# A two-block float32 transformer on one core: weight splits around the norms, the order of held products, and which queue carries the other transfers

## The chip, the cores and the metric

The kernel runs on one core of one Trainium2 chip. The metric is the device time of one execution in microseconds (us); lower is better. The core's engines run side by side and meet through semaphores: PE (TensorE) multiplies, DVE (VectorE) and ACT (ScalarE) do elementwise work, POOL is GpSimd, SP (SyncE) only issues transfers. ACT and POOL can issue transfers as well, each in its own queue and in program order.

## The reference

256 tokens of width 1024 pass through two blocks, all in float32:

```python
for layer in range(2):                       # first block
    mix = diff_attention(x) if layer == 0 else stick_breaking(x)
    x = layer_norm(ALPHA * x + mix)
    x = layer_norm(ALPHA * x + peer(x))      # 16384 experts, 16 for each of 8 heads
u = rms_norm(x, attn_pre_norm)               # second block
h = x + rms_norm(hybrid_mixer(u), attn_post_norm)
u = rms_norm(h, mlp_pre_norm)
out = h + rms_norm(square(relu(u @ w_up)) @ w_down, mlp_post_norm)
```

`peer` scores keys, picks experts by two top-16 searches, weighs gelu(x·u) of the picked experts by a softmax and sums their rows of v. The kernel computes it densely: all 16384 rows of u and v, the weights of unpicked experts being zero.

## The kernel before, in words

**Weights as a stream.** All 740 weight tiles (128x1024 float32, 512 KB each) are used once, in the order of `plan`. `Stream.load` brings tile i into one of four `raw` buffers through SP's queue. `Stream.split` makes two float32r parts of it: `hi` by a cast on ACT (line 66), `lo = raw - hi` on DVE (line 67). The activations are split in the same way by `part` (lines 163 and 164), and each product is three matmuls: hi·hi, hi·lo and lo·hi. A raw buffer is free when its `lo` is made, and the next load waits for that. The parts sit in three common buffers (`PARTS`), or, for tiles named by `keep`, in buffers of their own, which need not wait for PE.

**Order.** Each engine works in the order in which the program issues to it. `Stream.next` hands out the tile that is due and, in passing, issues the loads up to three tiles ahead and the splits up to two ahead (plus `extra`), unless all three common buffers are taken.

**Phases.** There are seven: attention 0, peer 0, attention 1, peer 1, mixer, and the two halves of the MLP. Before most of them stands a norm over all 1024 columns, so PE must wait for the vector engines there. The tokens are two blocks of 128 (b = 0, 1). To cover the norm, the last products of a phase for block 1 are held back: for the last `defer` tiles PE does block 0 only, and then the held jobs, 6 matmuls each, for block 1, while DVE and ACT normalise block 0. Then PE transposes block 0 (line 289), does the first four tiles of the next phase for block 0 (`half_pass(0)`, 24 matmuls of 512 columns) while block 1 is normalised, transposes block 1 and does `half_pass(1)`. These four are the junction tiles; they have buffers of their own.

**Where splits are issued.** In `half_pass(0)` each of the four junction tiles is drawn with `next`, which splits two further ahead. In `proj_n` (attention and mixer outputs), `extra` lets all four junction tiles be split before the norm. In the value stage of `peer` (128 tiles of v) `extra` is 0, so two junction tiles are split before the norm, and two junction tiles and the first two tiles after them in `half_pass(0)`, which `layer_norm` issues after the whole norm of block 1.

**Norm.** `norm` adds the residual to the sum in PSUM by halves of 512 columns (line 305), takes mean and variance (308, 309), an inverse root (258 to 264, ACT and DVE in turn), then centres both halves and multiplies by the gain (313), then scales both and adds the bias (316). The second block uses `post_norm` and `pre_norm`, which begin with a sum of squares on ACT (908).

**Other transfers.** The residual `x` is written to DRAM between phases (`spill`) and read again, and gains, masks, tables and sub-keys are loaded, all in SP's queue among the weight tiles. H, the output of the experts' first half, goes out by SP and back in by ACT.

Of the kernel before, what the change touches and what calls it, by code (L numbers as in the profile page):

```python
# [15 lines left out]
ALU = mybir.AluOpType  # L16
# [19 lines left out]
class Stream:  # L36
# [33 lines left out]

    def next(self):

        i = self.used
        self.used += 1
        self.load(i + 1 + self.ahead)
        self.split(i + 1 + self.split_ahead + self.extra, i)
        got = self.cut[i]
        self.cut[i] = None
        return got
# [46 lines left out]
class Kernel:  # L126
# [49 lines left out]

    def mm_n(self, acc, xh, xl, hi, lo, start, stop):

        mm = self.nc.tensor.matmul
        for x, w, a, b in ((xh, hi, start, False), (xh, lo, False, False), (xl, hi, False, stop)):  # L180
            for half in range(2):
                mm(acc[half], x, w[:, half * 512 : half * 512 + 512], start=a, stop=b)  # L182

    def proj_n(self, xh, xl, count, pool, defer, ready=None):


        self.st.keep(count - defer, defer, pool)
        acc, held = None, []
        for k in range(count):
            while ready and not ready(k):  # L190
                self.bg.tick()
            if acc is None:
                acc = [[self.ps("acc") for _ in range(2)] for _ in range(NB)]
            self.st.extra = max(0, min(2, NJ * (k + 2 - count + defer) // defer))
            hi, lo = self.st.next()
            for b in range(NB):
                t = slice(b * P, b * P + P)
                job = (acc[b], xh[:, k, t], xl[:, k, t], hi, lo, k == 0, k == count - 1)
                if b == 0 or k < count - defer:
# [35 lines left out]
    def half_pass(self, b, tiles):  # L235
# [31 lines left out]
    def bcast(self, pool, src, tag):  # L267
        t = pool.tile([P, D], F32, tag=tag, name=f"{tag}{self.n}")
        self.n += 1
        self.nc.sync.dma_start(t, src.unsqueeze(0).to_broadcast([P, D]))  # L270
        return t

    def gains(self, pool, tag, *srcs, late=None):
        t = pool.tile([P, len(srcs), D], F32, tag=tag, name=f"gains{self.n}")
        self.n += 1
        for i, src in enumerate(srcs):
            load = lambda i=i, src=src: self.nc.sync.dma_start(t[:, i], src.unsqueeze(0).to_broadcast([P, D]))
            if late is None:
                load()
            else:  # L280
                late.append(load)
# [13 lines left out]
    def norm(self, pool, b, acc, x, g, beta):  # L295
# [70 lines left out]
    def layer0(self, pool_x):  # L366
        nc, tc, a = self.nc, self.tc, self.a
        with ExitStack() as ctx:
# [166 lines left out]
    def layer1(self, spill):  # L535
        nc, tc, a = self.nc, self.tc, self.a
        mm = nc.tensor.matmul
        with ExitStack() as ctx:
# [5 lines left out]
            mask = one.tile([P, W], F32, tag="mask", name="mask1")  # L544
            nc.sync.dma_start(mask, a["c_mask1"])
            tri = one.tile([P, 2, P], F32R, tag="tri", name="tri1")
            tri_in = one.tile([P, 2, P], F32, tag="tri_in", name="tri_in1")
            nc.sync.dma_start(tri_in, a["c_tri"])
            nc.scalar.copy(tri, tri_in)
# [58 lines left out]
            halves.add(0)  # L608
            nc.sync.dma_start(x, spill)
            for c in range(KD):  # L610
# [15 lines left out]
            j.close()  # L626
            nc.sync.dma_start(spill, x)


    def peer(self, layer, spill, begin):  # L630
# [15 lines left out]
        with ExitStack() as ctx:  # L646
# [5 lines left out]
            sk = rp.tile([P, 8, P], F32, tag="sk", name=f"sk{layer}")  # L652
            nc.sync.dma_start(sk.rearrange("p h n -> p (h n)"), a["sub_keys"][layer])
            nc.sync.dma_start(iota, a["c_iota"])
            nc.sync.dma_start(iotak, a["c_iotak"])
            IX = [rp.tile([P, 2, 16, 8], U16, tag=f"ix{b}", name=f"ix{layer}{b}") for b in range(NB)]
# [184 lines left out]
        with ExitStack() as ctx:  # L841
# [23 lines left out]
            for i in range(P):  # L865
# [8 lines left out]
                if i == P // 2:  # L874
                    xr = vx.tile([P, NB, D], F32, tag="xr", name=f"xr{layer}")
                    nc.sync.dma_start(xr, spill)
# [19 lines left out]
            nc.sync.dma_start(spill, xr)  # L896
            lctx.close()
# [68 lines left out]
    def block2(self, spill):  # L966
# [4 lines left out]
        with ExitStack() as ctx:  # L971
# [7 lines left out]
            sin = one.tile([P, NB, 16], F32, tag="sin", name="sin2")  # L979
            nc.sync.dma_start(cos, a["c_cos2"])  # L980
            nc.sync.dma_start(sin, a["c_sin2"])
            cv = one.tile([P, KD, 8], F32, tag="cv", name="cv2")
            nc.sync.dma_start(cv, a["cols2"])
            mask = one.tile([P, W], F32, tag="mask", name="mask2")
            nc.sync.dma_start(mask, a["c_mask2"])
            qk = [self.jd, kn]
# [193 lines left out]
            x = xp.tile([P, NB, D], F32, tag="x", name="x2")  # L1180
            nc.sync.dma_start(x, spill)
            gains = self.gains(xp, "gains", a["attn_post_norm_2"][0], a["mlp_pre_norm_2"][0])
# [10 lines left out]
        with ExitStack() as ctx:  # L1193
# [6 lines left out]
            for b in range(NB):  # L1200
                self.post_norm(two, acc[b], x[:, b], gains[0])
                u = self.pre_norm(two, x[:, b], gains[1])
                for h in range(2):
                    self.transposed(b, h, u)
                if b == 0:
                    self.half_pass(0, tiles)
            self.half_pass(1, tiles)
            nc.sync.dma_start(spill, x)
        j.close()
        outer.close()  # L1210
        with ExitStack() as ctx:
# [5 lines left out]
            x = one.tile([P, NB, D], F32, tag="x", name="x3")  # L1217
            nc.sync.dma_start(x, spill)
            gain = self.bcast(one, a["mlp_post_norm_2"][0], "gain")
# [25 lines left out]
def body(tc, a, stop="all"):  # L1245
    nc = tc.nc
    with ExitStack() as ctx:
        ctx.enter_context(tc.manual_schedule())
        k = Kernel(tc, ctx, a)
        with tc.tile_pool(name="xa", bufs=1) as px:  # L1250
# [4 lines left out]
            spill = k.dram.tile([P, NB, D], F32, tag="xs", name="xs")  # L1255
            nc.sync.dma_start(spill, x)
        k.peer(0, spill, lambda pool, late: None)
# [99 lines left out]
```

## Time and profile before

| | |
|---|---|
| median of 3 runs | 2309.69 us (2308.02 to 2313.12) |
| the profiled execution's own time | 2311.31 us |
| its span, first to last instruction | 2309.2 us |
| mean granted TensorE clock | 0.988 of full speed |
| busy: PE, DVE, ACT, POOL | 97%, 76%, 54%, 3% |
| moved by DMA | 479.85 MB, mean 208 GB/s |

The span is what the trace covers; 2.1 us of the execution lie outside it. A busy PE in this table is one with a matmul in flight: matmuls overlap, and one that runs at a reduced clock counts as busy for longer.

### The profile page before, as it was taken

What the parts mean: (1) busy time and instruction counts of PE and PEld (TensorE: products, weight loads), DVE (VectorE), ACT (ScalarE), POOL (GpSimd) and SP (SyncE); (2) the same over time, 40 slices, a digit from 0 to 9 for tenths busy, and PEclk for the clock granted to TensorE, in tenths of its full rate; (3) what the DMA queues carried; (4) which work ended last, traced back from release to release, by engine and by line L of the source; (5) the groups of instructions that cost most, each with busy time, mean ns of one, the idle gap of its engine ahead of it and who ended that gap; (6) DMA issues with size and microseconds to landing.
All of it is one profiled execution on the core that took longest, in us unless ns stands there. A gap on an engine that the chain in (4) does not pass through costs nothing.

```text
span 2309.2 us, 39787 instructions
## 1 busy us (share of the span) xinstructions
PE 2230.4 (97%) x15028; PEld 2011.0 (87%) x15028; DVE 1752.8 (76%) x3488; ACT 1237.7 (54%) x2128; POOL 58.3 (3%) x79
## 2 busy tenths in 40 slices
PE   7889999999999999999999999999999899998998
PEld 6769999999888888887999999888888779997987
DVE  5968999888766767576998988766666856676754
ACT  4545454666555444584445566655444546755543
POOL 5400000000000000000000000000000000000000
PEclk9999999999999999999999999999999999999999
DMA  6336667555777777545666655677777564464764
GB/s 209 120 129 226 226 228 241 191 200 203 259 241 259 241 245 252 167 132 179 229 228 229 226 191 201 234 241 243 258 244 249 199 194 149 137 206 142 227 195 142
DMA packets 150657, 479.85 MB, mean 208 GB/s; under 512 B 17728, under 2 KB 18624, under 8 KB 149184
## 3 DMA queue, kind: packets, MB, share of 16 engines
q1 hardware_dynamic: 131456, 442.69, 59.1%
q10 hardware_dynamic: 19008, 34.61, 4.0%
q8 instruction: 118, 1.93, 0.3%
q14 instruction: 75, 0.61, 0.1%
HBM read 437.39 MB, written 39.85 MB: 207 GB/s over the span
## 4 chain that ended last, share of the span: by engine, by line
PE 85%; DVE 6%; ACT 4%; DMA 2%; issue 2%; POOL 1%; SPq 0%; DVEq 0%; ACTq 0%; POOLq 0%
PE ps_acc L182 34%; PE ps_h L157 15%; PE ps_h L159 14%; PE ps_h L158 14%; DVE lo L67 2%; PE ps_acc L805 1%; PE ps_acc L806 1%; ACT hi L66 1%; PE ps_acc L158 1%; PE ps_acc L159 1%; PE ps_acc L157 1%; DMA raw<-w_up 1%; PE ps_acc L689 0%; DVE aa L469 0%; POOL swq L418 0%
## 5 line engine op out<-in xcount | busy, mean ns | idle before, releaser
L67 DVE TENSOR_TENSOR lo<-raw,hi 128x1024 fp32r<-128x1024 f32 x740 | 904.9, 1226 | 454.2 <-ACT hi L66 451.8
L66 ACT CAST hi<-raw 128x1024 fp32r<-128x1024 f32 x740 | 775.4, 1050 | 437.3 <-issue 308.6
L157 PE MATMUL ps_h<-xh,hi 128*128 128x256 f32 x2784 | 790.3, 284 | 5.0 <-ACT r L1237 2.2
L159 PE MATMUL ps_h<-xh,lo 128*128 128x256 f32 x2784 | 774.3, 278 | 1.3 <-DVE lo L67 1.1
L158 PE MATMUL ps_h<-xl,hi 128*128 128x256 f32 x2784 | 774.4, 278 | 0.0
L157 PEld LDWEIGHTS ps_h<-xh,hi 128*128 128x128 f32 x2784 | 526.5, 189 | 11.8 <-ACT r L1237 2.4
L159 PEld LDWEIGHTS ps_h<-xh,lo 128*128 128x128 f32 x2784 | 525.1, 189 | 2.3 <-DVE lo L67 2.3
L158 PEld LDWEIGHTS ps_h<-xl,hi 128*128 128x128 f32 x2784 | 525.3, 189 | 0.2
L182 PE MATMUL ps_acc<-hi,wh 128*128 128x512 f32 x1024 | 315.4, 389 | 3.3 <-ACT wh L163 3.3
L182 PE MATMUL ps_acc<-hi,wo 128*128 128x512 f32 x1024 | 315.4, 389 | 0.0
L182 PE MATMUL ps_acc<-lo,wh 128*128 128x512 f32 x1024 | 315.1, 389 | 0.0
L832 ACT ACTIVATE hs<-ps_h 128x256 f32<-128x256 f32 x256 | 98.3, 384 | 344.1 <-PE ps_h L159 176.2
L182 PEld LDWEIGHTS ps_acc<-hi,wh 128*128 128x128 f32 x1024 | 192.1, 188 | 43.5 <-ACT wh L163 3.6
L182 PEld LDWEIGHTS ps_acc<-hi,wo 128*128 128x128 f32 x1024 | 192.3, 188 | 39.9
L182 PEld LDWEIGHTS ps_acc<-lo,wh 128*128 128x128 f32 x1024 | 192.3, 188 | 39.7
L164 DVE TENSOR_TENSOR wo<-jd,wh 128x256 fp32r<-128x256 f32 x256 | 107.2, 419 | 2.0 <-ACT wh L163 2.0
L856 DVE TENSOR_TENSOR jd<-G,jd 128x256 f32<-128x256 f32 x256 | 106.9, 418 | 2.2 <-ACT G L808 2.2
L163 ACT CAST wh<-jd 128x256 fp32r<-128x256 f32 x256 | 101.7, 397 | 10.4 <-DVE jd L856 10.4
L808 ACT ACTIVATE G<-ps_acc 128x64 f32<-128x64 f32 (+1 forms) x256 | 82.0, 385 | 6.6 <-PE ps_acc L806 1.0
L157 PE MATMUL ps_h<-hi,xh 128*128 128x512 f32 x160 | 70.8, 442 | 11.8 <-ACT hi L66 9.8
L158 PE MATMUL ps_h<-lo,xh 128*128 128x512 f32 x160 | 67.9, 424 | 5.7 <-DVE lo L67 5.7
L159 PE MATMUL ps_h<-hi,xl 128*128 128x512 f32 x160 | 68.0, 425 | 2.5 <-DVE xl L164 2.5
(323 smaller groups left out, 2384.3 us busy)
## 6 DMA issues: line engine op xcount, KB each, us to landing
raw<-peer_u SPq DMA_DIRECT2D x256, 512.0 KB, 4.5
raw<-peer_v SPq DMA_DIRECT2D x256, 512.0 KB, 4.3
H<-hs SPq DMA_DIRECT2D x128, 256.0 KB, 2.1
jd<-H ACTq DMA_DIRECT2D x128, 256.0 KB, 4.2
raw<-w_in SPq DMA_DIRECT2D x32, 512.0 KB, 3.7
raw<-w_up SPq DMA_DIRECT2D x32, 512.0 KB, 4.4
raw<-w_down SPq DMA_DIRECT2D x32, 512.0 KB, 3.7
raw<-w_qkv SPq DMA_DIRECT2D x24, 512.0 KB, 4.5
```

The lines of the kernel that those rows point to most:

```text
L66: self.nc.scalar.copy(hi, raw)
L67: self.nc.vector.tensor_sub(lo, raw, hi)
L157: mm(out, lh, rh, start=start, stop=False)
L158: mm(out, lh, rl, start=False, stop=False)
L159: mm(out, ll, rh, start=False, stop=stop)
L163: self.nc.scalar.copy(hi, src)
L164: self.nc.vector.tensor_sub(lo, src, hi)
L182: mm(acc[half], x, w[:, half * 512 : half * 512 + 512], start=a, stop=b)
L805: mm(out, o[:, 0, j], o[:, 1, j], start=True, stop=False)
L808: nc.scalar.activation(gt[:, :, 4 * g : 4 * g + 4], ps.rearrange("p (t i) -> p i t", t=4)[:, first:end], AF.Copy, scale=1.0 / GSCALE,)
L832: nc.scalar.activation(hs[i // 2][:, i % 2], o, AF.Gelu)
L856: nc.vector.tensor_tensor(w, g[:, i - first], hl[i // 2][:, i % 2], ALU.mult)
```

## The change

Five edits.

1. **Value stage.** From the 116th of the 128 v tiles `extra` is 1, from the 120th 2, so that all four junction tiles are split in the value stage. In `proj_n` the formula for `extra` becomes `k - count + 6`, whatever `defer` is.
2. **Between the norms.** `half_pass(0)` draws its tiles with `calm=True`, which splits no further than the tile itself; before it stands a call that splits all four where that isn't done. `half_pass(1)` splits the next three tiles, one before each of its second, third and fourth steps.
3. **Held products.** `finish` does all held jobs for the first 512 columns, then all for the second.
4. **Norm.** The second half is centred after the first half is finished, not before.
5. **Transfers.** All transfers but weight tiles, H, the first constants and the output go from SP's queue to POOL's (`nc.gpsimd.dma_start`).

```diff
-    def next(self):
+    def next(self, calm=False):
         ...
-        self.split(i + 1 + self.split_ahead + self.extra, i)
+        self.split(i + 1 if calm else i + 1 + self.split_ahead + self.extra, i)
-    def mm_n(self, acc, xh, xl, hi, lo, start, stop):
+    def mm_n(self, acc, xh, xl, hi, lo, start, stop, halves=range(2)):
         ...
-            for half in range(2):
+            for half in halves:
+    def finish(self, held):
+        for half in range(2):
+            for job in held:
+                self.mm_n(*job, (half,))
 # proj_n
-            self.st.extra = max(0, min(2, NJ * (k + 2 - count + defer) // defer))
+            self.st.extra = max(0, min(2, k - count + 6))
         ...
-        for job in held:
-            self.mm_n(*job)
+        self.finish(held)
 # half_pass
             if b == 0:
-                tiles.append(self.st.next())
+                tiles.append(self.st.next(calm=True))
+            elif j:
+                self.st.split(self.st.used + j, self.st.used)
 # norm
-        for s in halves:
-            nc.vector.scalar_tensor_tensor(y[:, s], y[:, s], mv[:, 0:1], g[:, s], ALU.subtract, ALU.mult)
+        centre = lambda s: nc.vector.scalar_tensor_tensor(y[:, s], y[:, s], mv[:, 0:1], g[:, s], ALU.subtract, ALU.mult)
+        centre(halves[0])
         next(root)
         for s in halves:
+            if s is halves[1]:
+                centre(s)
             nc.vector.scalar_tensor_tensor(x[:, b, s], y[:, s], r, beta[:, s], ALU.mult, ALU.add)
 # layer_norm, ahead of half_pass(0); the same in block2
+        self.st.split(self.st.used + NJ, self.st.used)
 # peer, value stage
+                if i >= GSPLIT:
+                    self.st.extra = min(2, (i - GSPLIT) // 4)
                 hi, lo = self.st.next()
         ...
-            for job in held:
-                self.mm_n(*job)
+            self.st.extra = 0
+            self.finish(held)
 # layer0, and so for gains, bcast, mask, tri_in, sk, iota, iotak, xr, cos, sin, cv, x and spill elsewhere
-            nc.sync.dma_start(x, a["x"].rearrange("(b p) d -> p b d", p=P))
+            nc.gpsimd.dma_start(x, a["x"].rearrange("(b p) d -> p b d", p=P))
```

## Rows read from the trace of the kernel before

**Rows 1.** The page, busy time, share and count by engine.
```profile
PE 2230.4 (97%) x15028; PEld 2011.0 (87%) x15028; DVE 1752.8 (76%) x3488; ACT 1237.7 (54%) x2128; POOL 58.3 (3%) x79
```

**Rows 2.** Windows over three junctions: length, busy by engine, PE clock, DMA.
```profile
905.00:945.00 40.00, 35.39 (x155) 27.77 (x154) 28.90 (x49) 14.85 (x25) 0.00 (x0) 0.96 0.53 177
1795.00:1860.00 65.00, 58.07 (x239) 45.45 (x238) 47.52 (x94) 30.38 (x52) 0.14 (x2) 0.92 0.54 180
2098.00:2150.00 52.00, 41.53 (x223) 34.57 (x222) 30.21 (x58) 24.84 (x50) 0.00 (x0) 0.90 0.46 162
```

**Rows 3.** Timeline of PE, peer 0 to attention 1: start, length, [idle before].
```profile
929.33 0.50 PE L157 MATMUL ps_h<-hi,xh 128*128 128x512 f32 x1 [1.53 <-ACT hi L66]
932.44 0.73 PE L158 MATMUL ps_h<-lo,xh 128*128 128x512 f32 x1 [2.60 <-DVE lo L67]
```

**Rows 4.** Timeline of DVE in the same junction.
```profile
915.41 1.27 DVE L305 SCALAR_TENSOR_TENSOR lny<-xr,ps_acc 128x512 f32<-128x512 f32 x2
...
923.18 0.69 DVE L305 SCALAR_TENSOR_TENSOR lny<-xr,ps_acc 128x512 f32<-128x512 f32 x1 [1.58 <-PE ps_acc L182]
924.46 0.69 DVE L164 TENSOR_TENSOR xl<-ps_m,xh 128x512 fp32r<-128x512 f32 x1 [0.59 <-ACT xh L163]
```

**Rows 5.** Timeline of ACT: the last value tiles, and the start of attention 1.
```profile
908.72 1.05 ACT L66 CAST hi<-raw 128x1024 fp32r<-128x1024 f32 x1 [0.95 <-DMA raw<-peer_v]
...
945.98 0.41 ACT L549 CAST tri<-tri_in 128x256 fp32r<-128x256 f32 x1
```

**Rows 6.** Timeline of SP there: spill, mask and table in its queue.
```profile
932.79 0.43 SPq L896 DMA_DIRECT2D xs<-xr  x1
...
939.64 0.43 SPq L548 DMA_DIRECT2D tri_in<-c_tri  x1
```

**Rows 7.** Timeline of PE, peer 1 to mixer.
```profile
1828.98 1.09 PE L289 MATMUL ps_m<-ident,pnu 128*128 128x128 f32 x8 [1.68 <-DVE pnu L925]
...
1844.25 1.06 PE L289 MATMUL ps_m<-ident,pnu 128*128 128x128 f32 x8 [0.93 <-DVE pnu L925]
...
1858.36 0.51 PE L158 MATMUL ps_acc<-lo,xh 128*128 128x512 f32 x1 [0.95 <-DVE lo L67]
```

**Rows 8.** Timeline of DVE in the same junction.
```profile
1819.87 1.27 DVE L305 SCALAR_TENSOR_TENSOR lny<-xr,ps_acc 128x512 f32<-128x512 f32 x2
...
1824.64 1.42 DVE L316 SCALAR_TENSOR_TENSOR xr<-lny,lnr,gains 128x512 f32<-128x512 f32 x2
...
1828.43 0.48 DVE L925 TENSOR_SCALAR pnu<-pnu,pnr 128x512 f32<-128x512 f32 x1
...
1837.00 4.62 DVE L67 TENSOR_TENSOR lo<-raw,hi 128x1024 fp32r<-128x1024 f32 x4
```

**Rows 9.** Timeline of PE, attention 0 to peer 0, and attention 1 to peer 1.
```profile
150.67 1.82 PE L289 MATMUL ps_m<-ident,x 128*128 128x128 f32 x8 [2.29 <-DVE x L316]
...
162.01 0.50 PE L159 MATMUL ps_h<-hi,xl 128*128 128x512 f32 x1 [1.09 <-DVE xl L164]
...
1065.93 0.50 PE L159 MATMUL ps_h<-hi,xl 128*128 128x512 f32 x1 [1.41 <-DVE xl L164]
```

**Rows 10.** Timeline of the mixer-to-MLP junction: DVE, PE, SP.
```profile
2115.77 2.36 DVE L67 TENSOR_TENSOR lo<-raw,hi 128x1024 fp32r<-128x1024 f32 x2 [0.26 <-ACT hi L66]
...
2125.05 1.94 PE L289 MATMUL ps_m<-ident,pnu 128*128 128x128 f32 x8 [3.77 <-DVE pnu L925]
...
2134.53 0.33 SPq L1218 DMA_DIRECT2D x<-xs  x1
...
2145.64 0.39 PE L157 MATMUL ps_h<-xh,hi 128*128 128x256 f32 x1 [2.20 <-ACT r L1237]
```

**Rows 11.** Timeline of DVE at the end of the program.
```profile
2301.95 1.41 DVE L938 TENSOR_TENSOR qnu<-ps_acc,gain 128x512 f32<-128x512 f32 x2 [4.03 <-ACT msj L908]
```

**Rows 12.** Rows of the page's transfers, and POOL's tile in attention 0.
```profile
x<-x SPq DMA_DIRECT2D x1, 1024.0 KB, 6.1
L418 POOL TENSOR_TENSOR swq<-zq,sin x32: 712/733/1692, 26.1 to 90.8; 32x256 f32<-32x256 f32 x32
```

More of the change, by code (lines that the diff above doesn't have):

```diff
@@ L269, in bcast @@
         self.n += 1
-        self.nc.sync.dma_start(t, src.unsqueeze(0).to_broadcast([P, D]))
+        self.nc.gpsimd.dma_start(t, src.unsqueeze(0).to_broadcast([P, D]))
         return t
@@ L276, in gains @@
         for i, src in enumerate(srcs):
-            load = lambda i=i, src=src: self.nc.sync.dma_start(t[:, i], src.unsqueeze(0).to_broadcast([P, D]))
+            load = lambda i=i, src=src: self.nc.gpsimd.dma_start(t[:, i], src.unsqueeze(0).to_broadcast([P, D]))
             if late is None:
@@ L544, in layer1 @@
             mask = one.tile([P, W], F32, tag="mask", name="mask1")
-            nc.sync.dma_start(mask, a["c_mask1"])
+            nc.gpsimd.dma_start(mask, a["c_mask1"])
             tri = one.tile([P, 2, P], F32R, tag="tri", name="tri1")
             tri_in = one.tile([P, 2, P], F32, tag="tri_in", name="tri_in1")
-            nc.sync.dma_start(tri_in, a["c_tri"])
+            nc.gpsimd.dma_start(tri_in, a["c_tri"])
             nc.scalar.copy(tri, tri_in)
@@ L608, in layer1 @@
             halves.add(0)
-            nc.sync.dma_start(x, spill)
+            nc.gpsimd.dma_start(x, spill)
             for c in range(KD):
@@ L626, in layer1 @@
             j.close()
-            nc.sync.dma_start(spill, x)
+            nc.gpsimd.dma_start(spill, x)
     def peer(self, layer, spill, begin):
@@ L652, in peer @@
             sk = rp.tile([P, 8, P], F32, tag="sk", name=f"sk{layer}")
-            nc.sync.dma_start(sk.rearrange("p h n -> p (h n)"), a["sub_keys"][layer])
-            nc.sync.dma_start(iota, a["c_iota"])
-            nc.sync.dma_start(iotak, a["c_iotak"])
+            nc.gpsimd.dma_start(sk.rearrange("p h n -> p (h n)"), a["sub_keys"][layer])
+            nc.gpsimd.dma_start(iota, a["c_iota"])
+            nc.gpsimd.dma_start(iotak, a["c_iotak"])
             IX = [rp.tile([P, 2, 16, 8], U16, tag=f"ix{b}", name=f"ix{layer}{b}") for b in range(NB)]
@@ L875, in peer @@
                     xr = vx.tile([P, NB, D], F32, tag="xr", name=f"xr{layer}")
-                    nc.sync.dma_start(xr, spill)
+                    nc.gpsimd.dma_start(xr, spill)
                 if i >= GSPLIT and (i - GSPLIT) % 4 == 2 and late:
@@ L895, in peer @@
             self.layer_norm(tp, acc, xr, gb, bb, extra(tp, xr) if extra else None)
-            nc.sync.dma_start(spill, xr)
+            nc.gpsimd.dma_start(spill, xr)
             lctx.close()
@@ L979, in block2 @@
             sin = one.tile([P, NB, 16], F32, tag="sin", name="sin2")
-            nc.sync.dma_start(cos, a["c_cos2"])
-            nc.sync.dma_start(sin, a["c_sin2"])
+            nc.gpsimd.dma_start(cos, a["c_cos2"])
+            nc.gpsimd.dma_start(sin, a["c_sin2"])
             cv = one.tile([P, KD, 8], F32, tag="cv", name="cv2")
-            nc.sync.dma_start(cv, a["cols2"])
+            nc.gpsimd.dma_start(cv, a["cols2"])
             mask = one.tile([P, W], F32, tag="mask", name="mask2")
-            nc.sync.dma_start(mask, a["c_mask2"])
+            nc.gpsimd.dma_start(mask, a["c_mask2"])
             qk = [self.jd, kn]
@@ L1180, in block2 @@
             x = xp.tile([P, NB, D], F32, tag="x", name="x2")
-            nc.sync.dma_start(x, spill)
+            nc.gpsimd.dma_start(x, spill)
             gains = self.gains(xp, "gains", a["attn_post_norm_2"][0], a["mlp_pre_norm_2"][0])
@@ L1205, in block2 @@
                 if b == 0:
+                    self.st.split(self.st.used + NJ, self.st.used)
                     self.half_pass(0, tiles)
             self.half_pass(1, tiles)
-            nc.sync.dma_start(spill, x)
+            nc.gpsimd.dma_start(spill, x)
         j.close()
@@ L1217, in block2 @@
             x = one.tile([P, NB, D], F32, tag="x", name="x3")
-            nc.sync.dma_start(x, spill)
+            nc.gpsimd.dma_start(x, spill)
             gain = self.bcast(one, a["mlp_post_norm_2"][0], "gain")
@@ L1255, in body @@
             spill = k.dram.tile([P, NB, D], F32, tag="xs", name="xs")
-            nc.sync.dma_start(spill, x)
+            nc.gpsimd.dma_start(spill, x)
         k.peer(0, spill, lambda pool, late: None)
```

## The prediction, made before the result was known

> **What bounds the kernel now.** I read the page's busy times first: PE has a matmul in flight for 97% of the span [rows 1], with a fixed list of matmuls that the change does not touch. So time is to be had only where PE waits or runs at its lower clock. The timeline of PE, read for its idle times, shows them at the junctions. The windows put sizes on three of them [rows 2]: PE is idle for 4.6 of 40 us, 6.9 of 65 and 10.5 of 52, and the mean granted clock is 0.96, 0.92 and 0.90. The clock has two levels, 2.4 and 1.2 GHz, so a mean of 0.90 over 52 us is 10.4 us at the lower one, in which PE does half the work: 5.2 us lost beside the idle time, and 5.2 and 1.6 us in the other two windows. Then I took the timelines of DVE and ACT at each junction to see what stood ahead of the late instruction. It is mostly splits: PE waits for hi and lo of junction tiles that were issued behind block 1's norm [rows 3], for a pre-norm behind four lo [rows 7, 8], for xl behind two lo of the next phase [rows 9], or for a post-norm behind two [rows 10]. So the working goes junction by junction.
>
> **The change part by part.** *Peer 0 to attention 1.* The splits leave half_pass(0), and with them the idle 1.53 and 2.60 [rows 3] and the fall of the clock behind them (1.6): -5.7. But the two splits now stand ahead of block 0's norm on DVE. Four lo take 4.62 [rows 8], so two take 2.3, which is the lower bound of how late that norm starts. The loads may add to it: in this stretch ACT already waited 0.95 once for a tile [rows 5], and tiles are now asked for faster. Two such waits make the upper bound, 4.2. I take 3.1, between them, since only the last tiles can outrun the loads. What hides it: behind block 0's norm DVE sat idle for 1.58, until the held products were done, and for 0.59 [rows 4]. That covers 2.2, and 0.9 stays (0.1 to 2.0): -4.8 in all.
>
> The earlier end of the held half (edit 3) gives nothing here or at any other junction: DVE comes to that sum after the products are done. Edit 4 brings the first half of x one operation earlier, 0.7 (two take 1.42 [rows 8]), but the third matmul behind the transposes needs xl, which DVE makes after both halves of x; here that takes the gain.
>
> *The table of attention 1.* ACT casts tri at 945.98 [rows 5]; the copy of the first k is queued behind it, and with it a PSUM bank that PE needs for its third projection. The table was asked for 6.9 us after the spill was issued (932.79 to 939.64 [rows 6]), because its memory was the spill's source. Block 1's norm, and so the spill, comes no earlier, while ACT reaches the cast some 5 us earlier. PE's first two projections cover part. How long GpSimd takes to issue a transfer is in no row; nothing, if it issues as SP does and the cover is enough, and 4 us, the whole lead less about 1, are the ends. I take +1.6, nearer to the lower end, as two projections are about that much work.
>
> *Peer 1 to mixer.* The same two splits: late by 2.6 (2.3 to 3.5; the norm was started by a late load here already). Nothing hides it, since PE waits 1.68 for the pre-norm as it is [rows 7]. Then the four lo between block 1's norm and its pre-norm go: 4.6 [rows 8], less 0.4 of the pre-norm's squares on ACT that ran beneath them; the pre-norm's own 2.85 (1826.06 to 1828.91 [rows 8]) remains. The second transposes come at +2.6 - 4.6 + 0.4 = -1.6. half_pass(0) begins 2.6 later but no longer stalls for its tiles, so PE is through with it sooner and waits some 2 us for them in place of 0.93 [rows 7]. That may bring the lower clock, as it followed the idle times of attention 1's junction at a price of 1.6: 0 to 1.6, I take 0.9. And the wait of 0.95 for lo at the start of the mixer [rows 7] goes, as those tiles are split in half_pass(1): -0.9. Together -1.6 (-2.5 to +1).
>
> *Attention 0 to peer 0, attention 1 to peer 1.* The idle 1.09 and 1.41 before L159 [rows 9] were lo of the next phase ahead of xl; they go to half_pass(1), whose products outlast them. Edit 4 takes 0.7 from the idle 2.29 before the transposes, and one split that moves to an earlier step 0.2; in the second, of which less reaches PE, 0.5. -2.0 and -1.9 (each +-1, with the clock).
>
> *Mixer to MLP.* The norm of block 0 starts where it did: the order among its splits is the same. For block 1 two lo, 2.36, stood ahead of the post-norm [rows 10]: -2.4 of the idle 3.77, and 1.4 is left. With that the second stretch at the lower clock, about half of this window's 5.2 lost, shortens or goes: -1.6 (0 to -2.6). The wait of 2.20 at 2145.64 [rows 10] is a weight tile whose load was queued on SP behind x, and x was issued only at 2134.53, when half_pass(1) had freed its memory; on POOL's queue only the gain stands behind x: -2.2. Together -6.2.
>
> By the Trainium skill's page "DMA: Bandwidth & Descriptors", section "Issuing engines are not separate DMA queues", all queues run on the same 16 engines and another issuer saves only the issue time. By that alone these 2.2 would stay and the sum would be 2.2 smaller. What the row shows is a wait ahead of an issue, which bandwidth does not set, so I count them.
>
> *End and start.* At the end the first half of block 1 is done 18 matmuls earlier, so one of two squares and one of two products (1.41 for both [rows 11]) leave the tail: -0.7. At the start the load of x, on SP behind the first weight tiles, has no transfer ahead of it on POOL and meets the first weights and x transposed. It takes 6.1 for itself [rows 12]; half of that, 3.0, is the upper bound and nothing the lower. PE begins at the lower clock, where a delay costs half: +0.8.
>
> *Other transfers.* Residual, gains, masks and sub-keys within the long stages are covered by the weight tiles that are loaded three ahead; on POOL they go out as soon as their memory is free. If that cover fails, where the residual meets the first tiles of the two value stages, it costs up to 1 each; I take nothing. In the value stage the two further splits fall into DVE's spare time (76% busy [rows 1]); their price at its end is counted above.
>
> **Sum.** -4.8 + 1.6 - 1.6 - 2.0 - 1.9 - 6.2 - 0.7 + 0.8 = -14.8. From the profiled execution's own 2311.3 that is 2296.5. That execution lies 1.6 above the median of the runs shown, so a median would be near 2295; I say 2296.
>
> **Rivals.** *GpSimd's transfers come late* (the other side). Between 26 and 91 us one instruction of POOL takes between 712 and 1692 ns [rows 12] at the same size, so POOL can be held up while DVE works. If what it issues lands D later than from SP, four places pay, as their consumers stand in order on an engine that PE waits for: the table of attention 1 (ACT), cos and sin of the mixer (DVE), and the sub-keys of both peers (PE itself). With about 2 us of cover each, the cost is 4 x (D - 2): the whole gain is gone at D = 5.7, and at 8 the time is 2311.3 - 14.8 + 24 = 2320. For it: nothing in this trace says what D is. Against: DVE idles often at the junctions. I give it 6%. The Trainium skill's page "SBUF — State Buffer", sections "SBUF: two separate sides" and "Who interferes with whom", states why it could be: GpSimd writes descriptors through a port pair that it shares with DVE, and cannot while DVE runs in a two-port mode; it advises the queues of ACT or SP. No run here shows that yet.
>
> *The value stage only exchanges one wait for another.* If the loads cannot follow, the norm is late by 4.2 at both value ends. Then peer 0 gives -3.7 + 1.6, peer 1 +1, and PE's longer wait for the transposes costs the lower clock twice, 1.6 each. With the other terms (-10.0) the sum is -7.9: about 2303. For it: ACT's wait for a load in just this stretch [rows 5]. Against: one wait of 0.95 only. 22%.
>
> *Nothing comes of it*: PE's waits go where they were, but DVE, now the last at each junction, opens others of the same size and the lower clock follows them; 2307 to 2311. Against: DVE is idle for 24% of the span, and at the MLP junction its work gets shorter, not later. 9%, of which 1 for slower.
>
> The forecast keeps 63%: 2290 to 2302 by its own terms. The range of 2288 to 2304 takes in most of the second rival and leaves out the first, the third and the tails. A change under 0.2%, 4.6 us, is about what a measurement of this kernel can't tell from none. Faster than that: 0.85, the same 0.08, slower 0.07.
>
> **What would show it.** Right: no wait for hi or lo in half_pass(0) of attention 1's start; block 0's norm starting 2.3 to 4.2 later against the end of its products at both value ends; the idle time before L159 gone at both entries to peer; the idle before the second transposes of the MLP junction at about 1.4; no wait for r at the MLP's third tile; a wait of ACT for tri_in. Wrong: DVE or ACT waiting several us for anything issued by POOL, idle time of PE within a value stage, or half-clock stretches as long as before.

## The result, and the profile after

The changed kernel takes 2296.96 us (median of six executions, 2292.23 to 2298.80) against 2309.0 for the kernel before, run beside it: a ratio of 0.9939, 95% interval 0.9924 to 0.9955. The forecast was 2296 (2288 to 2304), faster by more than 0.2%. The profiled execution of the changed kernel took 2292.23, of which the trace spans 2290.5; it is the quickest of its six, 4.7 under their median, so part of what its trace shows is chance. A second profile, below, helps to tell which part.

The page's busy time after, against [rows 1]:

```profile
PE 2219.0 (97%) x15028; PEld 2000.7 (87%) x15028; DVE 1755.9 (77%) x3488; ACT 1239.7 (54%) x2128; POOL 77.3 (3%) x114
```

The matmuls are as many as before, and POOL has 35 more instructions, its transfers. PE is busy for 11.4 us less: it spends less time at the lower clock, and its matmuls of 256 columns were quicker by chance, as shown below. The windows that hold the work of [rows 2], with the same columns:

```profile
903.56:939.20 35.64, 34.85 (x160) 26.78 (x159) 30.42 (x52) 16.88 (x26) 2.93 (x6) 1.00 0.56 198
1785.69:1849.08 63.39, 57.74 (x238) 45.50 (x237) 49.88 (x99) 32.02 (x53) 2.81 (x7) 0.92 0.55 189
2086.18:2131.42 45.24, 38.82 (x223) 32.70 (x222) 32.28 (x59) 26.02 (x52) 1.59 (x3) 0.96 0.56 194
```

PE's idle time falls from 4.6 to 0.8 us in the first, little (6.9 to 5.7) in the second and from 10.5 to 6.4 in the third; the clock goes from 0.96, 0.92 and 0.90 to 1.00, 0.92 and 0.96.

Both kernels issue 15028 matmuls, and the order differs only among held products. So the start of the n-th matmul before, less its start after, is the lead that the changed kernel has there, and its growth over a stretch is what the stretch gave. The table has the stretches by the times of the kernel before, with the forecast's terms; plus is a gain, and the second profile is the one of the next section:

```
stretch (us, before)                     forecast   first profile   second profile
start, to 30                                -0.8         -2.8            -0.7
attention 0 to peer 0, 100 to 172           +2.0         +3.5            +2.2
peer 0 to attention 1, 900 to 940           +4.8         +5.0            +4.8
table of attention 1, 940 to 960            -1.6         -1.8            -1.5
attention 1 to peer 1, 1045 to 1070         +1.9         +1.4            +0.3
peer 1 to mixer, 1780 to 1865               +1.6         +1.6            -1.0
mixer to MLP, splits and norm, 2090 to 2141 +4.0         +3.8            +1.6
the same, wait for r, 2141 to 2150          +2.2         +2.9            +2.7
end, after 2295                             +0.7         +0.2            +0.2
all long stages between (six stretches)      0           +5.0            +0.2
sum                                        +14.8        +18.8            +9.0
```

The timeline of PE in the changed kernel, peer 0 to attention 1 [rows 3] and the start of attention 1, with all idle times over 0.2:

```profile
924.28 0.51 PE L157 MATMUL ps_h<-hi,xh 128*128 128x512 f32 x1 [0.24 <-ACT xh L163]
931.33 0.63 PE L296 MATMUL ps_m<-ident,xr 128*128 128x128 f32 x4 [0.48 <-DVE xr L325]
944.58 0.39 PE L157 MATMUL ps_h<-xh,hi 128*128 128x256 f32 x1 [1.28 <-ACT k L622]
```

The waits for hi and lo inside the first half pass, 1.53 and 2.60, are gone; the last line is new, the price of the table of attention 1. The same view, peer 1 to mixer [rows 7] (two lines) and mixer to MLP [rows 10] (two lines):

```profile
1822.06 1.97 PE L296 MATMUL ps_m<-ident,pnu 128*128 128x128 f32 x8 [3.16 <-DVE pnu L937]
1833.73 1.07 PE L296 MATMUL ps_m<-ident,pnu 128*128 128x128 f32 x8 [2.19 <-DVE pnu L937]
...
2100.95 1.97 PE L296 MATMUL ps_m<-ident,pnu 128*128 128x128 f32 x8 [3.96 <-DVE pnu L937]
2111.30 1.07 PE L296 MATMUL ps_m<-ident,pnu 128*128 128x128 f32 x8 [1.96 <-DVE pnu L937]
```

At peer 1 the idle times only moved: 1.68 to 3.16 ahead of block 0's transposes, 0.93 to 2.19 ahead of block 1's, and the wait of 2.61 for a lo inside the half pass, at 1838.27 in the kernel before, is gone. At the MLP 3.77 fell to 1.96 and the 2.20 for r is gone.

### The profile page after: what moved, and what is told of

The parts are those of the page before. It is cut to its first block, busy times and chain, and to the rows that moved or that the text cites. A ratio compares the mean times of both kernels' runs of the same rounds, so it can differ in the third digit from the quotient of the medians.

```text
span 2290.5 us, 39880 instructions
## 1 busy us (share of the span) xinstructions
PE 2219.0 (97%) x15028; PEld 2000.7 (87%) x15028; DVE 1755.9 (77%) x3488; ACT 1239.7 (54%) x2128; POOL 77.3 (3%) x114
## 4 chain that ended last, share of the span: by engine, by line
PE 82%; DVE 7%; issue 4%; ACT 4%; DMA 2%; POOL 1%; SPq 0%; ACTq 0%; DVEq 0%; POOLq 0%
PE ps_acc L182 31%; PE ps_h L157 14%; PE ps_h L159 14%; PE ps_h L158 14%; DVE lo L67 2%; ACT hi L66 1%; PE ps_acc L815 1%; PE ps_acc L816 1%; PE ps_acc L158 1%; PE ps_acc L157 1%; PE ps_acc L159 1%; DMA raw<-w_v 1%; PE ps_acc L699 0%; DVE aa L479 0%; POOL swq L428 0%
## 5 line engine op out<-in xcount | busy, mean ns | idle before, releaser
L163 ACT CAST wh<-jd 128x256 fp32r<-128x256 f32 x256 | 101.7, 397 | 10.6 <-DVE jd L866 10.5
L157 PE MATMUL ps_h<-hi,xh 128*128 128x512 f32 x160 | 69.0, 431 | 10.5 <-ACT hi L66 8.9
L815 PE MATMUL ps_acc<-oh 128*128 128x128 f16 x512 | 69.6, 221 | 0.0
L816 PE MATMUL ps_acc<-oh 128*128 128x128 f16 x512 | 68.6, 219 | 0.0
```

The source lines that it names most:

```text
L157: mm(out, lh, rh, start=start, stop=False)
L163: self.nc.scalar.copy(hi, src)
L815: mm(out, o[:, 0, j], o[:, 1, j], start=True, stop=False)
L816: mm(out, o[:, 0, j], o[:, 2, j], start=False, stop=True)
```

## Experiments

The theory: the gain is made at the junctions, by edit 2 above all (when splits are issued between the norms), and the queue pays at the MLP and costs at the start. The rivals: the queue carries it, or edit 1 does, or the splits only exchange one wait for another.

### Both kernels once more

No edit.

> The changed kernel once more, for a second profile and more times. Its first profile was the fastest of its six executions (2292.2 against a median of 2297.0) and leads the kernel before by 18.8 us, of which 13 to 14 lie at the junctions. The rest lies elsewhere: twice 1.3 in the key stages (experts' first half), 1.6 and 0.9 from two falls of the clock in the attention of layer 1 and the mixer that it does not have, and -0.9 in attention 0. Theory: these five are chance, so this profile has other values there and the same ones at the junctions (start +2.8, peer 0 to attention 1 -4.9 with +1.8 for the table, peer 1 to mixer -1.6, mixer to MLP -6.7, each within 0.5); median 2297 within 2. Rival: the 1.3 twice belong to the change, as other transfers left SP's queue, and come again.

> The kernel before once more, for a second profile. Theory: its junctions repeat to 0.3 us; what differs are falls of the clock and the rate of the 256-column matmuls at full clock, which was 113 ns each in some long stages and 118 in others, the same stage differing from execution to execution (up to 2.6 us in the first half of the MLP, 1.3 in a key stage). Rival: the rate belongs to the kernel (where its code or its tiles lie), so this profile has the same rate in each stage as the first of this kernel: 118 in the second part of both key stages, 113 in the MLP.

Measured: the changed kernel 2298.48 (2293.89 to 2301.99), ratio 0.9938 (0.9922 to 0.9954), profiled in 2301.99. The kernel before took 2316.53 in one execution. The second column of profiles above is this changed kernel against the first trace of before. Peer 0 (4.8), the table (1.5) and r (2.7) repeat within 0.4. The start, peer 1 to mixer and the splits at the MLP do not (-0.7, -1.0 and 1.6 in place of -2.8, 1.6 and 3.8), so the expectation that all junctions repeat within 0.5 failed at three of them. At peer 1 both profiles have the same time at the lower clock, and the norm of block 0 comes later in the second, as shown under the value stage. At the MLP the second has one more fall of the clock. Such falls follow the same idle time in one execution and not in the next; the windows of both profiles at attention 1 to peer 1, the first execution first:

```profile
1045.00:1060.00 15.00, 12.46 (x59) 9.31 (x59) 13.59 (x29) 4.71 (x10) 0.54 (x1) 1.00 0.20 75
```

```profile
1045.00:1060.00 15.00, 12.75 (x55) 9.71 (x54) 13.01 (x28) 4.96 (x10) 0.54 (x1) 0.89 0.23 94
```

Idle before the transposes was 1.19 and 0.87 in the first, 1.15 and 0.87 in the second; still one ran on at 1.00 and the other at 0.89 over 15 us. That is 15 x 0.11 = 1.7 us of work lost, more than the difference between +1.4 and +0.3. About half of the 9.8 between the two profiles is the rate of matmuls of 256 columns. Windows in the first half of the MLP, changed kernel (first and second execution), then before (first and second):

```profile
2131.50:2171.50 40.00, 40.00 (x356) 40.00 (x355) 29.66 (x46) 23.70 (x45) 0.00 (x0) 1.00 0.65 197
```

```profile
2139.00:2179.00 40.00, 40.00 (x342) 40.00 (x341) 28.10 (x44) 23.19 (x44) 0.00 (x0) 1.00 0.64 188
```

```profile
2150.00:2190.00 40.00, 40.00 (x355) 40.00 (x355) 30.64 (x47) 24.78 (x47) 0.00 (x0) 1.00 0.71 207
```

```profile
2153.00:2193.00 40.00, 40.00 (x342) 40.00 (x341) 28.02 (x43) 23.11 (x44) 0.00 (x0) 1.00 0.63 188
```

355 or 342 matmuls in 40 us, at the full clock and with PE never idle: one every 113 ns or every 117. Each kernel has had both rates in this stage, so the rate belongs to the execution; it is worth 2.5 us here and 1.3 in a key stage, where the first profile of the changed kernel was quick twice. So the rivals of both expectations fall: the 1.3 did not come again, and the kernel before did not keep its rates. But of the five differences that were taken for chance one came again: between 960 and 1045 the first profile gains 1.6 and the second 1.5. It goes with the table, as shown there.

### The load of x back on SP

```diff
 # layer0
-            nc.gpsimd.dma_start(x, a["x"].rearrange("(b p) d -> p b d", p=P))
+            nc.sync.dma_start(x, a["x"].rearrange("(b p) d -> p b d", p=P))
```

> Changed kernel, only the load of x in attention 0 back on SP's queue. Theory: on GpSimd's queue it goes out at 1.35 us and shares the engines with the first weight tiles, which costs PE 1.8 of idle time and a fall of the clock by 18.8 us; on SP it stands behind the first weight tiles, so PE's waits of 1.03 and 0.75 go and the time falls by 2.8, to about 2294. Rival: the first tiles are late for another reason, or x collides on SP as well; 2297 and the same two waits.

Measured: 2294.93 (2291.16 to 2298.68), ratio 0.9929 (0.9912 to 0.9945). By the medians it is 2.0 to 3.6 quicker than the changed kernel; by the intervals it can't be told from it. The traces tell more. PE's waits at the start in the changed kernel, first profile (two lines) and second (one):

```profile
17.05 0.51 PE L157 MATMUL ps_h<-hi,xh 128*128 128x512 f32 x1 [1.03 <-ACT hi L66]
18.31 0.50 PE L158 MATMUL ps_h<-lo,xh 128*128 128x512 f32 x1 [0.75 <-DVE lo L67]
```

```profile
17.77 0.50 PE L158 MATMUL ps_h<-lo,xh 128*128 128x512 f32 x1 [0.29 <-DVE lo L67]
```

With x on SP there is none after the first 10 us of this stage. In the changed kernel x goes out at 1.35 us, among the first weight tiles, and takes 11.5 to land where it took 6.1 [rows 12]. Leads at 20 us over the first trace of before: with x on SP +0.5 to +0.7 in four other kernels and -0.4 in the second profile of before; with x on POOL -0.4 to -0.7 in five profiles and -2.8 in the first. The means, without that one, are +0.3 (six profiles, the first of before at 0 among them) and -0.6: the usual price is about 0.9 us, and the 2.8 that the theory took from one profile was mostly chance.

### All transfers back on SP

`nc.gpsimd.dma_start` becomes `nc.sync.dma_start` in all 20 places; edits 1 to 4 stay.

> Changed kernel with all transfers of edit 5 back on SP's queue; edits 1 to 4 stay. Theory: the queue gives 2.2 to 2.9 at the MLP's third tile (a wait for r that comes back) and takes 2.8 at the start; the table of attention 1 is worth no more than 1 either way: 2297 within 2. Rival A, the queue carries more of the gain (the key stages' 1.3 twice, weight tiles no longer held up behind other transfers): 2300 or more. Rival B, GpSimd's issue costs time at each junction: 2294 or less.

Measured: 2301.01 (2296.91 to 2303.36), ratio 0.9949 (0.9933 to 0.9964). By the medians rival A has the size, 2.5 to 4 us for the queue, though the intervals overlap; it does not have the place that it named, the key stages. The trace shows four places: r at the MLP, the start of the mixer, the start of the program and the table of attention 1. PE's wait for r at the MLP is back, and two waits at the start of the mixer:

```profile
1851.61 0.51 PE L157 MATMUL ps_acc<-hi,xh 128*128 128x512 f32 x1 [0.79 <-ACT hi L66]
1852.87 0.50 PE L158 MATMUL ps_acc<-lo,xh 128*128 128x512 f32 x1 [0.75 <-DVE lo L67]
...
2134.18 0.39 PE L157 MATMUL ps_h<-xh,hi 128*128 128x256 f32 x1 [2.37 <-ACT r L1250]
```

SP's own timeline says why: at both places four weight tiles stand behind transfers that waited for memory or for the spill.

```profile
1842.63 0.33 SPq L992 DMA_DIRECT2D cos<-c_cos  x1
...
1845.70 1.86 SPq L50 DMA_DIRECT2D raw<-w_qkv  x4
...
2122.92 0.33 SPq L1231 DMA_DIRECT2D x<-xs  x1
2123.29 0.43 SPq L277 DMA_DIRECT2D gain<-mlp_post_norm  x1
2123.76 2.25 SPq L50 DMA_DIRECT2D raw<-w_up  x4
```

Against the second profile of the changed kernel the two profiles differ by 4.5 in the stretch of r (a fall of the clock of 1.7 in it) and 1.7 at peer 1 to mixer for the queue, and by 1.3 at the start and 1.5 at the table against it: 3.5 in all at these four places (the two spans differ by 1.3 alone, as other stretches went the other way). The table is a place where POOL's queue loses. In the changed kernel POOL issues it after the mask, and ACT waits; the timelines of POOL and of ACT, and the table's KB and time to landing:

```profile
936.81 0.54 POOL L555 DMA_DIRECT2D mask<-c_mask  x1 [4.79 <-DMA xs<-xr]
937.34 0.54 POOL L558 DMA_DIRECT2D tri_in<-c_tri  x1
```

```profile
943.85 0.41 ACT L559 CAST tri<-tri_in 128x256 fp32r<-128x256 f32 x1 [4.28 <-DMA tri_in<-c_tri]
```

```profile
tri_in<-c_tri POOLq DMA_DIRECT2D x1, 128.0 KB, 6.3
```

With all queues back on SP (its timeline, then ACT's, then the transfers' KB and time to landing):

```profile
933.51 0.43 SPq L558 DMA_DIRECT2D tri_in<-c_tri  x1
```

```profile
937.36 0.41 ACT L559 CAST tri<-tri_in 128x256 fp32r<-128x256 f32 x1
```

```profile
tri_in<-c_tri SPq DMA_DIRECT2D x1, 128.0 KB, 2.3
```

2.3 us to landing in place of 6.3, and no wait. The weight tiles that SP's queue held back there had been issued ahead of the table in the changed kernel.

### The table alone on POOL, and the table on SP

In the first, the load of x and of both gains of attention 1 go back to SP, mask and table stay on POOL. In the second, the load of x in attention 0 and that of the table go to SP:

```diff
 # table alone: layer1
-            nc.gpsimd.dma_start(x, spill)
+            nc.sync.dma_start(x, spill)
         ...
 # table (and x of layer0, as above) on SP: layer1
-            nc.gpsimd.dma_start(tri_in, a["c_tri"])
+            nc.sync.dma_start(tri_in, a["c_tri"])
```

> Changed kernel with the load of x and of the two gains of attention 1 on SP's queue, so that mask and table are the only transfers that GpSimd issues there. In the changed kernel the table landed 6.1 to 6.3 us after its issue, as the second of five in a row; from SP's queue 2.3. Theory: the five share what carries them, so alone the table lands in 3 to 4 and PE's wait for k is below 0.3. Rival: GpSimd is late with it whatever follows (its issue, or DVE's work beside it): 5.5 or more and PE's wait of about 1 stays.

> Changed kernel with two transfers back on SP's queue: the load of x in attention 0 and the table of attention 1; the other transfers stay on GpSimd's. Theory: from GpSimd's queue the table landed 6.1 to 6.3 us after its issue, from SP's 2.3 (all queues back) to 3.4, and with all queues back ACT's cast of it kept PE waiting for nothing; so the wait for k (1.07 to 1.28) goes and with it 1.5 us at the start of attention 1, beside the 1 to 3 of x at the start: about 2293.5. Rival: the table waits for the spill to land, whatever the queue, and PE's wait stays at 1 us: 2295, as with x alone.

Measured, table alone: one execution of 2298.36; PE's wait for k is 1.84. Its transfers and ACT's cast stand as in the rival: 6.6 us to landing. But neither reading fits: x, issued from SP at 935.32, lands ahead of it after 4.8. The transfers:

```profile
x<-xs SPq DMA_DIRECT2D x1, 1024.0 KB, 4.8
raw<-w_q SPq DMA_DIRECT2D x2, 512.0 KB, 7.4
...
mask<-c_mask POOLq DMA_DIRECT2D x1, 192.0 KB, 6.3
tri_in<-c_tri POOLq DMA_DIRECT2D x1, 128.0 KB, 6.6
```

Here, in the changed kernel and with the queues back, transfers land nearly in the order in which they were issued, whichever queue they came from; POOL reaches the mask 0.9 after the spill has landed, and by then x and a weight tile are ahead. That a transfer is not slow because GpSimd issues it shows at the start of the mixer, where at most one weight tile is under way: a mask of 192 KB lands about as soon from either queue (changed kernel, then queues back).

```profile
mask<-c_mask POOLq DMA_DIRECT2D x1, 192.0 KB, 2.6
```

```profile
mask<-c_mask SPq DMA_DIRECT2D x1, 192.0 KB, 2.3
```

Measured, table on SP: 2294.98 (2290.27 to 2297.53), ratio 0.9930 (0.9917 to 0.9944). The table lands in 2.1, ACT does not wait, and the stretch from 940 to 960 loses nothing (the changed kernel: 1.5 to 1.8). In the median the 1.5 over x alone is not to be seen; intervals of 3 us to either side could not show it.

And part of the 1.5 is given back later. In all twelve profiles PE idles for the same 2.1 us near 1025 (times of before). Where PE has waited for k (five profiles), and in one more, the one without edits 3 and 4, its clock then stays at 1.00 and the stretch from 960 to 1045 gains 1.5 to 1.6. In the other six the clock falls there, and the stretch gains nothing. The windows over that place, x alone on SP and then x and table on SP, which differ in the table's queue alone:

```profile
1010.00:1030.00 20.00, 17.90 (x93) 15.42 (x93) 15.60 (x27) 15.29 (x28) 0.00 (x0) 1.00 0.34 101
```

```profile
1010.00:1030.00 20.00, 17.90 (x87) 15.45 (x86) 14.03 (x24) 13.97 (x27) 0.00 (x0) 0.91 0.32 89
```

In four of the six profiles without that fall one comes at the next junction, attention 1 to peer 1, where the stretch then gives -0.3 to 0.3 in place of 1.1 and 1.4. So from 940 to 1070 the six give 0.1 to 1.2 in sum, and the three kernels with edit 2 and the table on SP 1.5 to 2.2. Why a loss of 0.4 to 2.2 us at the table does away with a fall of the clock 80 us later, no run shows.

The kernel with x and table on SP and the one with x alone there have lower medians than the changed kernel and are the quickest versions found, though their intervals overlap its own.

### The splits undone, and edit 2 alone

In the first, edits 1 and 2 are undone. In the second, edit 2 alone is put into the kernel before:

```diff
 # edit 2 alone; next takes calm as in the change
         ...
-                tiles.append(self.st.next())
+                tiles.append(self.st.next(calm=True))
+            elif j:
+                self.st.split(self.st.used + j, self.st.used)
 # layer_norm and block2, ahead of half_pass(0)
+        self.st.split(self.st.used + NJ, self.st.used)
```

> Changed kernel with edits 1 and 2 undone: splits are issued where they were before; held products by halves, norm and queues stay as changed. Theory: the splits are most of the gain: +4.9 at peer 0 to attention 1 less 1.7 of the table's wait, +1 to 2 at each entry to a peer, +1.6 at peer 1 to mixer, +3 to 4 at mixer to MLP: +10 to +12, so 2307 to 2309. Rival (the value stage only exchanges one wait for another, and the splits between norms only move DVE's work): 2301 or less.

> Kernel before with edit 2 alone: calm draws in half_pass(0), the call that splits all four junction tiles ahead of it, three further tiles in half_pass(1). Value stage, held products, norm and queues as before. Theory: this is the part that carries the gain: 1 at each entry to a peer (no lo of the next phase ahead of xl), 4 at peer 0 to attention 1 without the table's wait, 0 to 1 at peer 1 to mixer, 3 to 4 at mixer to MLP, where the wait for r stays: 9 to 11 of the 12 to 14, so 2299 to 2302. Rival: it needs edit 1 (junction tiles split ahead of the norm) or the queue to pay; 2304 or more.

Measured: 2307.51 without the splits (2304.66 to 2312.01, ratio 0.9984, 0.9974 to 0.9993), 2298.75 with edit 2 alone (2298.37 to 2302.59, ratio 0.9952, 0.9940 to 0.9965). The theory held in both (edit 2 alone is even 0.25 us under its bracket): edits 1 and 2 are three quarters of the gain, 0.46% of 0.62, and edit 2 without any other makes 0.48%. Without the splits the waits of [rows 3] are back:

```profile
928.51 0.50 PE L157 MATMUL ps_h<-hi,xh 128*128 128x512 f32 x1 [1.53 <-ACT hi L66]
931.75 0.51 PE L158 MATMUL ps_h<-lo,xh 128*128 128x512 f32 x1 [2.74 <-DVE lo L67]
```

With edit 2 alone, other transfers on SP, the start of the mixer still has a wait for lo of 0.76, and the MLP one for r of 1.65.

### The value stage without edit 1

```diff
                 if i >= GSPLIT:
-                    self.st.extra = min(2, (i - GSPLIT) // 4)
+                    self.st.extra = 0
```

> Changed kernel with edit 1 undone in the value stages alone: no splits further ahead there, so two junction tiles are split between the norms of the two blocks (two lo, 2.4 us) and not before the first norm. Edit 2 stays. Theory: in the last six steps of the value stage PE needs 1.36 us a step and DVE 1.81 with a lo in each, so the further two lo make PE fall behind (0.8 to 1.4 at peer 0, 1.9 at peer 1) and delay the norm by about 3; without them the first norm starts earlier, and the two lo delay the second block's pre-norm by 2.4 in its place: net -1 to +1 at each end, so 2295 to 2299; edit 2 carries nearly all of the gain at the value ends. Rival: edit 1 carries it, and hi or lo of junction tiles make PE wait in the first half pass again: 4 to 8 slower, 2301 to 2305.

Measured: 2296.52 (2292.58 to 2299.01), ratio 0.9937 (0.9925 to 0.9950): the same as the changed kernel, as the theory had it. Against PE's work (its start, plus the lead that PE had before the last steps of the stage, less the start in before) the norm of block 0 starts 0.7 later than in the kernel before at both peers, where the changed kernel starts it 3.0 and 3.1 later at peer 0 and 2.3 and 4.4 at peer 1 (its two profiles). PE's waits, peer 0 (two lines) and peer 1 (two lines):

```profile
928.13 0.63 PE L296 MATMUL ps_m<-ident,xr 128*128 128x128 f32 x4 [1.74 <-DVE xr L325]
929.58 0.63 PE L296 MATMUL ps_m<-ident,xr 128*128 128x128 f32 x4 [0.82 <-DVE xr L325]
...
1820.47 1.09 PE L296 MATMUL ps_m<-ident,pnu 128*128 128x128 f32 x8 [2.17 <-DVE pnu L937]
1833.96 1.94 PE L296 MATMUL ps_m<-ident,pnu 128*128 128x128 f32 x8 [6.03 <-DVE pnu L937]
```

Two lo stand ahead of the norm or behind it, and PE waits ahead of block 0's transposes or of block 1's. The stretch at peer 0 gives 4.0 where the changed kernel gives 4.8 to 5.0, that at peer 1 +0.4 where five profiles with edit 1 and these transfers on POOL give 1.6, -1.0, 1.0, 2.3 and 0.3. What edit 1 costs shows in the value stage, in ACT's timeline of the changed kernel, where ACT waits for loads:

```profile
901.55 1.05 ACT L66 CAST hi<-raw 128x1024 fp32r<-128x1024 f32 x1 [0.81 <-DMA raw<-peer_v]
...
904.32 1.05 ACT L66 CAST hi<-raw 128x1024 fp32r<-128x1024 f32 x1 [1.42 <-DMA raw<-peer_v]
```

Split faster, the tiles outrun their loads; DVE then has no slack over the last steps, in which PE does block 0 alone. DVE makes a lo in each, one every 1.81 us, and PE's last steps come at that pace (changed kernel, two lines) where they came every 1.36 in before (two lines):

```profile
911.40 0.73 PE L182 MATMUL ps_acc<-hi,wh 128*128 128x512 f32 x2
...
913.21 0.73 PE L182 MATMUL ps_acc<-hi,wh 128*128 128x512 f32 x2
```

```profile
908.24 0.62 PE L182 MATMUL ps_acc<-hi,wh 128*128 128x512 f32 x2
...
909.60 0.62 PE L182 MATMUL ps_acc<-hi,wh 128*128 128x512 f32 x2
```

So PE loses 1.2 us of its lead between 900 and 915 without a single long wait; without edit 1 it loses nothing there. That the loads set it off is read from ACT's waits; no run tests the loads by themselves.

### Held products and norm as before

Edits 3 and 4 undone: held jobs one after the other, both halves centred together.

> Changed kernel with edits 3 and 4 undone: held products job by job, both halves of the norm's second step centred before the first is finished. Theory: the first half of x comes 0.7 later at the five layer norms (seen where PE waits for it: both entries to a peer and peer 0 to attention 1), and the tail of the end is 0.7 longer: 1.5 to 3 slower, 2298 to 2300. Rival: DVE is late at each junction anyway, so that nothing changes: 2297 within 1.

Measured: 2298.73 (2293.69 to 2299.72), ratio 0.9946 (0.9934 to 0.9959). The median lies in the theory's bracket, 0.3 to 1.8 above the changed kernel's two, but the intervals can't tell the kernels apart. The first half of x does come earlier with edit 4 (attention 0 to peer 0, ahead of the transposes: PE idles for 1.43 and then 0.80 in the second profile of the changed kernel, and for 2.07 at once with the edits undone), but the sum is the same within 0.2. At the end the trace after the last matmul is 0.4 longer without edit 3.

## Why the prediction was right, point by point

**Right in place and, but for what is said here, in size.** *Peer 0 to attention 1*: 4.8 forecast, 4.6 to 5.1 in six profiles with all of edits 1 to 4. Block 0's norm is late by 3.1 as forecast (3.0 and 3.1), but what that costs came by another way. PE itself loses 1.2 of it in the last steps of the value stage, where the forecast let the two splits fall into DVE's spare time; against the end of its products the norm is 1.8 late, under the forecast's 2.3, and the held products hide nearly all of it. That 1.2 came in place of the forecast's 0.9 is luck. *Mixer to MLP*: 6.2 in sum, 6.8 and 4.3 measured (one more fall of the clock in the second); the idle time ahead of block 1's transposes fell to 1.96 where 1.4 was forecast. The wait for r hung on the queue alone, as shown by both kernels with the other transfers on SP (2.37 and 1.65) and by its absence without the splits but with POOL. *Entries to the peers*: 2.0 and 1.9. At the first 2.2 were measured in the second profile (3.5 in the first, without a fall of the clock that before has). At the second it was 1.1 to 2.3 in five profiles without a fall of the clock there, and -0.3 to 0.3 in four with one, under the forecast's bound of 0.9: the waits for xl went, but a fall of the clock could take back all of it. *Edits 3 and 4*: next to nothing at the junctions. *Peer 1 to mixer*: a gain of 1.6 (2.5 to -1), measured -1.0 to +2.3; the stall is exchanged for a wait of 2 us, as forecast, and how late the loads leave the norm (2.3 to 4.4, forecast 2.6) decides the sign. Here the second rival is half right: one wait is exchanged for another. *Start*: -0.8, usually -0.9, once -2.8.

**Right in size, wrong in cause.** *The table of attention 1*: 1.6 forecast, 1.5 to 1.8 measured in the changed kernel. The forecast's step was that ACT reaches the cast 5 us earlier while the spill comes no earlier, and that GpSimd's queue adds nothing. On SP's queue the wait is nil with the same lead; so it is the queue: weight tiles overtake the table once SP no longer waits for the spill ahead of them. The fall of the clock near 1025 that goes with this wait was in no term. From 940 to 1070, table and entry to peer 1 together, the forecast has 0.3 and the six profiles have 0.1 to 1.2; that this fits is luck too. *The wait for lo at the start of the mixer*: it was put down to splits that move to half_pass(1); with those in place and the transfers on SP it was 0.76 (edit 2 alone) or two of 0.79 and 0.75 (queues back), with POOL nil or 0.42, and 0.40 with POOL but without those splits. So most of it is the queue's.

**Mis-sized.** *End*: -0.7 forecast, 0.2 measured to before and 0.4 to the kernel without edit 3: DVE's last product is half as long but begins 0.81 after the last matmul in place of 0.53, as it waits for ACT's square. *Other transfers*: nothing, where the start of the mixer gives some 1.7 by two single profiles. The two err in opposite directions. Two of the signs by which the forecast wanted to be called wrong did appear: ACT waited 4.28 for a transfer that POOL issued, and PE lost time within a value stage. Each cost 1.2 to 1.8 us, so they did not decide the sum.

**The rivals.** GpSimd's transfers do come late at one place, by about 4 us at the table, near the 5.7 at which four places together would have taken the whole gain. The other three did not pay. The rival that nothing comes of the change falls with the times. That one wait is only exchanged for another holds for edit 1, not for edit 2.

**The rule on queues.** The Trainium skill's "DMA: Bandwidth & Descriptors", section "Issuing engines are not separate DMA queues", says that all queues end in the same 16 engines. The trace agrees, in that a table of 128 KB from another queue still lands behind what was issued before it (6.3 us, against 2.3 when it went first). But the 2.2 to 2.9 at the MLP are real: another queue changes who is issued first, and with it who waits. The Trainium skill's "SBUF — State Buffer", section "Who interferes with whom", lets GpSimd's descriptors wait for DVE. That is not what made the table late: DVE had nothing to do while it was under way, as its timeline shows.

```profile
934.70 2.35 DVE L67 TENSOR_TENSOR lo<-raw,hi 128x1024 fp32r<-128x1024 f32 x2
945.51 1.23 DVE L67 TENSOR_TENSOR lo<-raw,hi 128x1024 fp32r<-128x1024 f32 x1 [8.45 <-ACT hi L66]
```

Only the 0.9 between the landing of the spill and the issue of the mask, while DVE made its last lo, could be of that kind; no run tells.

## What to carry to other kernels

At a junction, list what stands on DVE between the last product and the first that needs the norm; work for the next phase that needn't be done there is moved behind. That edit alone was worth 0.48%. Moving work ahead into a stage on the strength of DVE's spare time over the whole span (24%) paid nothing here, where the last steps of the stage are shorter than the others. Moving transfers to another queue is a change of order: look at what will now be issued ahead of each of them, not only at what it frees.

## What was not expected of the hardware

Matmuls of 128x256 came every 113 or every 117 ns at the same granted clock of 1.00, with PE and its weight loads both busy throughout; the rate was constant through the first half of the MLP and differed between executions of one kernel. In each key stage it makes 1.3 us, in the MLP 2.5. The same idle time was followed by a fall of the clock (1.7 us) in one execution and not in another; near 1025 it went with PE's wait for k 80 us before, in eleven of twelve profiles. Together with chance in the loads they spread the executions of either kernel over some 10 us, nearly the whole gain, so a difference of two single profiles is read stretch by stretch. What sets the rate, and what decides such a fall, stays open.
